# A hybrid layer on one core: norm weights on the gathered rows, another order of the last chunks' routing, overflow rows transposed one product later

## The chip, the cores and the metric

The kernel runs on one core of a Trainium2 chip. The metric is the device time of one execution in microseconds (us). A core has five engines, each with its own instruction queue: PE (TensorE, matrix products; PEld is its loading of the stationary operand), DVE (VectorE), ACT (ScalarE), POOL (GpSimd) and SP (SyncE, which here only starts transfers). ACT and POOL start transfers too. An engine works through its queue in order and waits on semaphores of the others.

## The reference

The input is 512 tokens of 1024 numbers. A normalized input goes through one combined projection into a stick-breaking attention and a gated spatial mix; both go through the output projection and are added to `h`. What the change touches is the second half:

```
hn = rmsnorm(h, ffn_norm_g)                 # h * rsqrt(mean(h*h)) * g
g_logits = hn @ w_router_group + b_g        # 4 groups: the best one
e_logits = hn @ w_router_expert + b_e       # 8 experts in it: the best two
h = h + sum over the token's two experts of
        gate * (silu(hn @ w_gate[e]) * (hn @ w_up[e])) @ w_down[e]
out = rmsnorm(h, final_norm_g)
```

There are 32 experts; `w_gate`, `w_up` and `w_down` hold 2 MB each per expert in float32, 201 MB in all.

## The kernel before

**Routing.** The tokens are four chunks `c` of 128 and `h[:, c]` is finished in two halves `n` by the output projection. The loop `for u in range(9)` does one half of one chunk per step and runs the letters of the string `U1[u]` in order, through `u_step`. The letters: `o` and `O` are the products of the output projection (tile `o`), `A` adds them to `h`; `q` squares the half before (`sqj`) and after its second half makes the row scale `rs2` (DVE, then a power on POOL); `t` transposes it on PE (`pt`) and ACT copies it out (`hT`); `l` is the product with the router weights (`lg`); `g` is `with_gain`, `h` times the norm weights `ffB`, on POOL and in step 8 on DVE; `s` is `store_xn`, which scales these rows by `rs2` on ACT and stores them to `xn_d` in DRAM; `r` and `R` run the next instructions of a chunk's routing on DVE (`route`: a chain of reductions over `L`, `em` to the two one-hot rows `oab`, at its end the `code` rows, on ACT for the last two chunks); `m`, `p`, `M` place the tokens (`pos_mm`, `positions`, `rows_mm`). After the loop the whole chain of chunk 3 runs (`go(16, R[3])`), gives the row list `gi`, and POOL gathers the first rows from `xn_d` into `xg`.

**Experts.** Sixteen pairs `p` of experts follow, 64 slots for each expert. For pair `p` PE does `gu(a)` and `gu(b)` (gate and up, tile `gu`), transposes the results (`act`, tile `ft`; ACT and DVE make `hg`), adds the pair before into `h` (`combine`, tiles `cb`), transposes the next pair's gathered rows (`prep_pair`, tiles `px`, evicted to `xs` by ACT and DVE), and does `down(p)` (tile `y`). Tokens beyond 64 of an expert, at most 32 in all, go through a second path: `over_2` gathers them into `xgo` in pair 0, `prep(xso, xgo, "o")` transposes them (`pxo`, to `xso`), and branches (`if_over`) use `xso` in the pairs that need it. At the end their sum `yo` is spread over the tokens with a one-hot tile `oho` and added in `unit`.

**What sets the order.** Each engine's order is the program's order. Weights come in 1 MB halves on SP's queue (`load_next`); a half can start when the slot that it takes is free, that is, when the products that read it last are done, and SP starts them strictly in order.

Of the kernel before, what the change touches and what calls it, by code (L numbers as in the profile page):

```python
# [8 lines left out]
F32 = mybir.dt.float32  # L9
F32R = mybir.dt.float32r  # L10
# [3 lines left out]
OP = mybir.AluOpType  # L14
# [39 lines left out]
)  # L54
U1 = (
# [9 lines left out]
)  # L65
F1 = 7
NSB = 4
# [4 lines left out]
def layer_kernel(ctx, tc, xr, xT, gT, w_inT, w_inR, sgg, wsT, bsp, sbg, sog, w_out, ffp, ffg, wr, br,  # L72
# [4 lines left out]
    def bcast(ap2d, cols):  # L77
        return bass.AP(tensor=ap2d.tensor, offset=ap2d.offset, ap=[[0, P], [1, cols]])
# [611 lines left out]
    dma(ffgs, ffg)  # L690
    brB = rw.tile([P, 36], F32, name="brB")
    dma(brB, bcast(br, 36))
    ffB = rw.tile([P, KD, P], F32, name="ffB")
    dma(ffB, bcast(ffp, D))
    load_next(2)
    slots[:0] = [half_slot(ringc)] * 4
    load_next(4)
# [35 lines left out]
        else:  # L733
            rsqrt(rs2[:, c:c + 1], msh[:, 1, c:c + 1], 1, msh[:, 0, c:c + 1])

    def with_gain(c, n, eng):

        if n == 0:
            xn[c] = rw.tile([P, KD, P], F32, tag="xn", bufs=2, name=f"xn{c}")
        ps_ = slice(n * 64, (n + 1) * 64)  # L740
        eng.tensor_tensor(xn[c][:, :, ps_], h[:, c, n * 512:(n + 1) * 512].rearrange("t (p k) -> t k p", k=KD),
                          ffB[:, :, ps_], op=OP.mult)

    def store_xn(c):
        nc.scalar.activation(xn[c], xn[c], AF.Copy, scale=rs2[:, c:c + 1])
        nc.scalar.dma_start(xn_d[c * P:(c + 1) * P], xn[c])

    def turn(c, n):
# [102 lines left out]
    def u_step(x, u):  # L851
        c, n = divmod(u, 2)
        pc, pn = divmod(u - 1, 2)
        if x == "o" and u < 8:
            bank1.append(op_.tile([P, 512], F32, tag="o", name=f"o1_{n}_{c}"))
            wo_mm(bank1[-1], 1, n, c, 0, 1)
        elif x == "O" and u < 8:
            wo_mm(bank1[-1], 1, n, c, 2, 3)
        elif x == "A" and u < 8:
            wo_add(bank1[-1], 1, n, c)  # L860
        elif x in "rR" and u >= 3:
            k = (8 if u >= 7 else 4) if x == "r" else 4
            go(k, R[(u - 3) // 2])
        elif x == "q" and u > 0:
            square(pc, pn)
        elif x == "t" and u > 0:
            turn(pc, pn)
        elif x == "g" and u > 0:
            with_gain(pc, pn, nc.vector if u == 8 else nc.gpsimd)
        elif x == "m" and u >= 5 and u != 6:  # L870
            pos_mm(2 if u == 8 else (u - 5) // 2)
        elif x == "p" and u in (5, 8):
            for k in (0,) if u == 5 else (1, 2):
                positions(k)
        elif x == "w" and u == 0:
            for k in range(KD):
                nc.vector.tensor_scalar(wrs[:, k], wrs[:, k], ffgs[:, k:k + 1], None, op0=OP.mult)
        elif x == "l" and u > 0:
            logits(pc, pn)
        elif x == "s" and u in (3, 5, 7):  # L880
            if u == 7:
                load_next(2)
            store_xn((u - 3) // 2)
        elif x == "M" and u in (6, 8):
            rows_mm(sps, soh, (0,) if u == 6 else (1, 2))
        elif x == "a":
            pass
# [72 lines left out]
    def prep(xs, x, name):  # L960

        for n in range(2):
            px = bank(f"px{name}_{n}", 4, P)
            for k in range(4):
                kk = 4 * n + k
                nc.tensor.transpose(px[:, k], x[:, kk * P:(kk + 1) * P], identf)  # L966
            (nc.scalar.copy, nc.vector.tensor_copy)[n](xs[:, 4 * n:4 * n + 4], px[:, :, :xs.shape[2]])

    def prep_pair(p):
        XS[p] = mo.tile([P, KD, P], F32, tag="xs", name=f"xs{p}")  # L970
# [75 lines left out]
    def combine(p, *units):  # L1046
        for u in units:
            ps = bank(f"cb{p}_{u}", 512)
            add_rows(ps, p, u, True, True)
            into_h(ps, u)  # L1050
# [109 lines left out]
    for p in range(NP):  # L1160
        a, b = 2 * p, 2 * p + 1
        last = p == NP - 1
        gu(a)
        if p == 0:
            over_1()
            pst = bank("pst", 2, NP)
            for i in range(8):
                for r, rs_ in halves:
                    nc.tensor.matmul(pst[rs_], ohf[:, i], cf[:, i, :, r::2], start=i == 0, stop=i == 7,
                                     skip_group_check=True)  # L1170
            nc.vector.tensor_copy(tab[:, 1], pst[:, 1])
            for c in range(NCH):
                nc.vector.tensor_scalar(tabt[:, c], pst[:, 0], PAD - c * P, None, op0=OP.add)
            load_next(4)
        if last:
            act(a)
            combine(p - 1, 0, 1, 2, 3, 4, 5)
        gu(b)
        if p == 0:
            over_2()  # L1180
            clear(True)
            load_next(4)
        else:
            with if_over(66 + p):  # L1184
                gate_up_over(a)
                gate_up_over(b)
            load_next(8)
        if last:
            act(b)
            combine(p - 1, 6, 7)  # L1190
            places(p)
            down_over(p)
            break
        act(a)
        if p:
            combine(p - 1, 0, 1, 2, 3)
        act(b)
        if p:
            combine(p - 1, 4, 5, 6, 7)
        places(p)  # L1200
        prep_pair(p + 1)
        if p == 0:
            prep(xso, xgo, "o")
        down(p)
        if p:
            down_over(p)
        load_next(4)
        results(p)


    room = [slots.pop(0)(f"fin{i}") for i in range(3)]
# [2 lines left out]
    dma(finB, bcast(fing, D))  # L1214
    p = NP - 1
    clear(False)
    oho = mo.tile([P, T], F32R, tag="cf", name="oho")
    for c in range(NCH):
        nc.vector.tensor_scalar(tabot[:, c:c + 1], tabo[:, :1], float(-c * P), None, op0=OP.add)
    tokens(oho, tabot)  # L1220
    yo2 = mo.tile([P, 2, 512], F32R, tag="xs", name="yo2")
    for n, rs_ in halves:
        nc.scalar.activation(yo2[:SLOTS, n], yo[rs_], AF.Copy, scale=tabo[rs_, 1:2])
# [13 lines left out]

    def unit(c, n):
        ps = bank(f"cl{c}_{n}", 512)
        nc.tensor.matmul(ps, oho[:, c * P:(c + 1) * P], yo2[:, n], start=True, stop=False, skip_group_check=True)  # L1240
        add_rows(ps, p, 2 * c + n, False, True)
        into_h(ps, 2 * c + n)

    def gained(c):
# [31 lines left out]
    def big(e, nm, oh2, tf, xr_, a, b):  # L1276
# [15 lines left out]
        for n in range(2):  # L1292
            px = bank(f"p2{nm}_{n}", 4, P)
            for k in range(4):
                kk = 4 * n + k
                for i in range(8):
                    nc.tensor.matmul(px[:, k], xr_[i % NCH][:, kk * P:(kk + 1) * P], own[:, i], start=i == 0,
                                     stop=i == 7, skip_group_check=True)
            nc.vector.tensor_copy(x2[:, 4 * n:4 * n + 4], px)
        pg = []  # L1300
        for i in range(2):
            ps = bank(f"g2{nm}_{i}", F)
# [69 lines left out]
def lay_out(x, attn_norm_g, w_in, sg_norm_g, w_spatial, b_spatial, sb_out_norm_g, sg_out_norm_g, w_out,  # L1372
            ffn_norm_g, w_router_group, b_router_group, w_router_expert, b_router_expert,
            w_gate, w_up, w_down, final_norm_g):
    import numpy as np
    c = np.ascontiguousarray

    def cols(v, n):
        return c(v.reshape(n, P).T)

    xs = x.reshape(T, D)
    wr = np.concatenate([w_router_group[0]] + [w_router_expert[0, g] for g in range(4)], axis=1)
    br = np.concatenate([b_router_group[0], b_router_expert[0].reshape(-1)])
    return {
        "xr": c(xs),
        "xT": c(xs.T.reshape(KD, P, T).transpose(1, 0, 2)),
        "gT": cols(attn_norm_g[0], KD),
        "w_inT": c(w_in[0].reshape(KD, P, 20, P).transpose(1, 2, 0, 3)[:, [0, 4, 1, 5, 2, 6, 3, 7, 12, 13, 14, 15]]),
        "w_inR": c(w_in[0].reshape(KD, P, 5, 512).transpose(1, 2, 0, 3)[:, [2, 4]]),
        "sgg": cols(sg_norm_g[0], NCH),  # L1390
        "wsT": c(w_spatial[0].transpose(2, 0, 1)),
        "bsp": c(b_spatial[0]),
        "sbg": cols(sb_out_norm_g[0], NCH),
        "sog": cols(sg_out_norm_g[0], NCH),
        "w_out": c(w_out[0].reshape(2, NCH, P, D).transpose(0, 2, 1, 3)),
        "ffp": c(ffn_norm_g[0].reshape(P, KD).T.reshape(1, D)),
        "ffg": cols(ffn_norm_g[0], KD),
        "wr": c(wr.reshape(KD, P, 36).transpose(1, 0, 2)),
        "br": c(br.reshape(1, 36)),
        "w_gate": c(w_gate.reshape(E, P, KD * F)),  # L1400
        "w_up": c(w_up.reshape(E, P, KD * F)),
        "w_down": c(w_down.reshape(E, P, 4 * D)),
        "fing": c(final_norm_g.reshape(1, D)),
    }
# [19 lines left out]
```

## Time and profile before

| What | Value |
|---|---|
| three runs | 756.58, 756.64, 760.25 us; median 756.64 |
| the profiled execution | 759.56 us, span 757.7 us |
| PE, busy share of the span | 93% |
| DVE, ACT, POOL | 41%, 29%, 12% |
| DMA | 231.54 MB, mean 306 GB/s |

The profile is of one execution, whose span (first to last instruction) is 1.86 us shorter than its time. Busy shares are means over stages with different limits. PE is nearly always busy, while the DMA engines are full only in the second two thirds of the span, where the page shows 418 to 420 GB/s in slice after slice.

### The profile page before, as it was taken

To read this page: it belongs to the slowest core of one execution; us is meant where nothing else is said; L and a number is where in the kernel's file an instruction comes from. 1 tells how busy PE (TensorE), PEld (TensorE's weight loads), DVE (VectorE), ACT (ScalarE), POOL (GpSimd) and SP (SyncE) were. 2 spreads that over 40 slices of the span, in tenths; PEclk is the share of its full clock that TensorE was granted. 3 is DMA by queue.
4 is the path that set the end of the run, shared out by engine and by line. 5 is a ranking of instruction groups with operands and counts; after the bars stand their busy time and mean duration, and the time that the engine had idled before them with its cause. 6 is when DMAs were issued, how large, how long until landed. Compare 5 with 4: busy or idle time off the path is not lost. (4 is left out here: it accounts for less than half of the span.)

```text
span 757.7 us, 9140 instructions
## 1 busy us (share of the span) xinstructions
PE 702.8 (93%) x3426; PEld 395.7 (52%) x3426; DVE 308.4 (41%) x541; ACT 216.5 (29%) x332; POOL 92.7 (12%) x84
## 2 busy tenths in 40 slices
PE   8999999999999796999999998989999999898993
PEld 6776757678788642434434434344344344244441
DVE  5546748355667711314304303042143043041355
ACT  6564856555344311111111111011111111111114
POOL 0322212125144201000000000000000000000001
PEclk9989979899999698999999999999999999999997
DMA  8802010207439597699999999999999999999953
GB/s 289 321 19 93 1 55 29 84 17 277 192 153 422 200 385 297 260 421 416 420 419 419 418 419 420 420 419 419 418 419 420 418 418 420 419 418 421 409 222 115
DMA packets 42391, 231.54 MB, mean 306 GB/s; under 512 B 6226, under 2 KB 7890, under 8 KB 18258
## 3 DMA queue, kind: packets, MB, share of 16 engines
q1 hardware_dynamic: 39394, 224.33, 73.1%
q0 software_dynamic: 2352, 4.20, 1.5%
q10 hardware_dynamic: 576, 2.10, 0.7%
q8 instruction: 43, 0.70, 0.4%
q14 instruction: 26, 0.21, 0.1%
HBM read 230.74 MB, written 4.19 MB: 310 GB/s over the span
## 5 line engine op out<-in xcount | busy, mean ns | idle before, releaser
L980 PE MATMUL gu<-r,xs 128*64 128x512 f32 x1024 | 226.1, 594 | 9.0 <-DMA r<-w_up 4.4
L980 PEld LDWEIGHTS gu<-r,xs 128*64 128x64 f32 x1024 | 82.8, 137 | 150.1 <-issue 137.2
L1010 PE MATMUL y<-r,hg 128*64 128x512 f32 x512 | 114.5, 600 | 3.3 <-ACTq L1145 2.9
L992 DVE TENSOR_TENSOR hg<-ft,gg 128x256 f32<-128x256 f32 x32 | 13.4, 420 | 231.5 <-ACT gg L990 224.4
L986 ACT COPY sg<-gu 128x512 f32<-128x512 f32 x32 | 18.7, 585 | 221.3 <-PE gu L980 221.3
L1044 DVE TENSOR_TENSOR h<-cb,h 128x512 f32<-128x512 f32 x120 | 74.2, 680 | 0.0
L1010 PEld LDWEIGHTS y<-r,hg 128*64 128x64 f32 x512 | 35.5, 138 | 71.6 <-issue 62.2
L918 POOL DMA_INDIRECT xg<-xn_d,gi x16 | 16.4, 1028 | 383.7 <-PE px L966 376.7
L1031 DVE SCALAR_TENSOR_TENSOR yl<-y,tab,yh 128x512 fp32r<-128x512 f32 x32 | 23.8, 750 | 71.0 <-ACT yh L1030 69.6
L1038 PE MATMUL cb<-yh,oh 128*128 128x512 f32 x120 | 49.9, 416 | 0.0
L1038 PE MATMUL cb<-yl,oh 128*128 128x512 f32 x120 | 47.4, 395 | 0.0
L1030 ACT ACTIVATE yh<-y,tab 128x512 fp32r<-128x512 f32 x32 | 21.8, 687 | 86.8 <-PE y L1010 86.1
L116 PE MATMUL pT<-xhi,hl_w 128*128 128x512 f32 x80 | 34.3, 429 | 0.0
L118 PE MATMUL pT<-xhi,hl_w 128*128 128x512 f32 x80 | 33.0, 413 | 0.0
L117 PE MATMUL pT<-xlo,hl_w 128*128 128x512 f32 x80 | 33.0, 412 | 0.0
L111 POOL TENSOR_TENSOR hl_w<-wqk,hl_w 128x1024 fp32r<-128x1024 f32 x10 | 24.4, 2435 | 66.5 <-ACT hl_w L110 64.2
L116 PE MATMUL pR<-hl_w,xhi 128*128 128x512 f32 x64 | 26.1, 409 | 0.0
L117 PE MATMUL pR<-hl_w,xhi 128*128 128x512 f32 x64 | 25.6, 400 | 0.2 <-DVE hl_w L111 0.2
L998 PEld LDWEIGHTS ft<-identf,sg 128*128 128x128 f32 x128 | 14.6, 140 | 21.3 <-issue 16.2
L118 PE MATMUL pR<-hl_w,xlo 128*128 128x512 f32 x64 | 25.4, 397 | 0.0
L1038 PEld LDWEIGHTS cb<-yh,oh 128*128 128x128 f32 x120 | 22.6, 188 | 4.8 <-DVE h L1044 0.8
L998 PE MATMUL ft<-identf,sg 128*128 128x128 f32 x128 | 19.6, 277 | 5.6 <-PEq L1184 3.7
(264 smaller groups left out, 941.3 us busy)
## 6 DMA issues: line engine op xcount, KB each, us to landing
r<-w_gate SPq DMA_DIRECT2D x64, 1024.0 KB, 20.0
r<-w_up SPq DMA_DIRECT2D x64, 1024.0 KB, 19.9
r<-w_down SPq DMA_DIRECT2D x64, 1024.0 KB, 20.2
wqk<-w_inT SPq DMA_DIRECT2D x10, 512.0 KB, 4.7
wr<-w_inR SPq DMA_DIRECT2D x8, 512.0 KB, 6.8
wo<-w_out SPq DMA_DIRECT2D x8, 512.0 KB, 4.5
xt<-xT SPq DMA_DIRECT2D x8, 256.0 KB, 4.5
h<-xr SPq DMA_DIRECT2D x4, 512.0 KB, 10.7
```

The source lines that it names most:

```text
L111: (nc.gpsimd if pool else nc.vector).tensor_tensor(lo, src, hi.bitcast(F32), op=OP.subtract)
L116: nc.tensor.matmul(ps, lh, rh, start=first, stop=False)
L117: nc.tensor.matmul(ps, lh, rl, start=False, stop=False)
L118: nc.tensor.matmul(ps, ll, rh, start=False, stop=last)
L980: nc.tensor.matmul(ps[rs_], xs[:, k], w, start=k == 0, stop=k == KD - 1, skip_group_check=True)
L986: nc.scalar.copy(SG[e], GU[e].rearrange("s (p j) -> s j p", j=4))
L998: nc.tensor.transpose(ft[:, j], SG[e][:, j], identf)
L1010: nc.tensor.matmul(YS[p][n][rs_], HT[e][:, j], down_weights(e, j, n), start=j == 0, stop=j == 3, skip_group_check=True)
L1030: nc.scalar.activation(yh[:, cs], YS[p][n], AF.Copy, scale=tab[:, 1, p:p + 1])
L1031: nc.vector.scalar_tensor_tensor(yl[:, cs], YS[p][n], tab[:, 1, p:p + 1], yh[:, cs].bitcast(F32), op0=OP.mult, op1=OP.subtract)
L1038: nc.tensor.matmul(ps, OHT[p][:, c * P:(c + 1) * P], y[:, n * 512:(n + 1) * 512], start=first and i == 0, stop=last and i == 1, skip_group ...
L1044: nc.vector.tensor_tensor(h[:, c, cs], ps, h[:, c, cs], op=OP.add)
```

## The change

Rows are now stored without the norm weights: `with_gain` (letter `g`) is gone, and ACT scales `h` straight into `xn`, earlier in steps 3, 5 and 7. The weights are multiplied in where the gathered rows leave PSUM after their transpose, where the weight is one number per partition (`ffk`): four activations per pair on ACT for the first half, one product with a broadcast operand on DVE for the second. The 512 KB broadcast `ffB` becomes 4 KB `ffk`. In step 8 the routing of chunk 2 goes first on DVE up to its one-hots (`z`), and its `code` rows on ACT come after the square and the copy (`k`). The overflow rows are transposed in pair 1 between `gu(a)` and `gu(b)`, and `oho` is made in pair 2; in `unit` its product is the last of three instead of the first.

```
-    "o r R q t g m p O A w l s M a",
-    "r R q t g a m p l M",
+    "o s r R q t m p O A w l M a",
+    "z q t m k p l M",
...
-    ffB = rw.tile([P, KD, P], F32, name="ffB")
-    dma(ffB, bcast(ffp, D))
+    ffk = keep.tile([P, KD], F32, name="ffk")
+    dma(ffk, ffp)
...
-        eng.tensor_tensor(xn[c][:, :, ps_], h[:, c, n * 512:(n + 1) * 512].rearrange("t (p k) -> t k p", k=KD),
-                          ffB[:, :, ps_], op=OP.mult)
...
-        nc.scalar.activation(xn[c], xn[c], AF.Copy, scale=rs2[:, c:c + 1])
+        xn[c] = rw.tile([P, KD, P], F32, tag="xn", bufs=2, name=f"xn{c}")
+        nc.scalar.activation(xn[c], h[:, c].rearrange("t (p k) -> t k p", k=KD), AF.Copy, scale=rs2[:, c:c + 1])
...
+        elif x == "z":
+            go(3, R[2])
+        elif x == "k":
+            go(1, R[2])
...
-            (nc.scalar.copy, nc.vector.tensor_copy)[n](xs[:, 4 * n:4 * n + 4], px[:, :, :xs.shape[2]])
+            if n == 0:
+                for k in range(4):
+                    nc.scalar.activation(xs[:, k], px[:, k, :xs.shape[2]], AF.Copy, scale=ffk[:, k:k + 1])
+            else:
+                nc.vector.tensor_tensor(xs[:, 4:], px[:, :, :xs.shape[2]],
+                                        ffk[:, 4:, None].to_broadcast([P, 4, xs.shape[2]]), op=OP.mult)
...
+        if p == 1:
+            prep(xso, xgo, "o")
         gu(b)
...
-        if p == 0:
-            prep(xso, xgo, "o")
         down(p)
...
+        if p == 2:
+            oho = mo.tile([P, T], F32R, tag="cf", name="oho")
+            for c in range(NCH):
+                nc.vector.tensor_scalar(tabot[:, c:c + 1], tabo[:, :1], float(-c * P), None, op0=OP.add)
+            tokens(oho, tabot)
...
-        nc.tensor.matmul(ps, oho[:, c * P:(c + 1) * P], yo2[:, n], start=True, stop=False, skip_group_check=True)
-        add_rows(ps, p, 2 * c + n, False, True)
+        add_rows(ps, p, 2 * c + n, True, False)
+        nc.tensor.matmul(ps, oho[:, c * P:(c + 1) * P], yo2[:, n], start=False, stop=True, skip_group_check=True)
```

On ACT, in step 8 of the routing loop, this stood before:

```order
L797 ACTIVATE code<-oab,tlocf 128x2x32
L798 ACTIVATE code<-oab 128x2x32
L729 ACTIVATE sqj,msh<-h 128x512
L754 COPY hT_1_1962<-pt_1_1957 128x512
L745 ACTIVATE xn_1924<-xn_1924,rs_1620 128x1024
L746 DMA xn_d<-xn_1924 128x1024
```

And this stands there now:

```order
L729 ACTIVATE sqj,msh<-h 128x512
L748 COPY hT_1_1952<-pt_1_1947 128x512
L791 ACTIVATE code<-oab,tlocf 128x2x32
L792 ACTIVATE code<-oab 128x2x32
L739 ACTIVATE xn_1987<-h,rs_1620 128x1024
L740 DMA xn_d<-xn_1987 128x1024
```

The two `code` rows of chunk 2 have moved behind the last square and the last copy; the store of chunk 3 reads `h` itself.

On PE, at the end of pair 0, this stood before, between the transposes of pair 1's rows and `down(0)`:

```order
L966 MATMUL px_1_2315<-identf,xg 128x128 x4
L966 MATMUL pxo_2324<-identf,xgo 128x128 x4
L966 MATMUL pxo_2330<-identf,xgo 128x128 x4
L1010 MATMUL y_0_2336<-r_2_0_1599,hg_2295 64x512
L1010 MATMUL y_0_2336<-r_2_0_1601,hg_2304 64x512
```

And now the overflow rows stand in pair 1, behind the last product of `gu(a)` and ahead of the first of `gu(b)`:

```order
L981 MATMUL gu_2354<-r_1_1_1892,xs_2303 64x512
L962 MATMUL pxo_2373<-identf,xgo 128x128 x4
L962 MATMUL pxo_2382<-identf,xgo 128x128 x4
L981 MATMUL gu_2388<-r_0_0_1985,xs_2303 64x512
L981 MATMUL gu_2388<-r_1_0_2063,xs_2303 64x512
```

The eight transposes are the same; `down(0)` and `gu(a)` of pair 1 now come before them. SP's order of weight halves is the same in both.

## Rows read from the trace of the kernel before

**Rows 1.** Busy time by stretch: PE, PEld, DVE, ACT, POOL, clock, DMA share, GB/s.

```profile
284.90:292.80 7.90, 1.88 (x10) 1.58 (x10) 1.61 (x3) 0.70 (x2) 1.59 (x2) 0.69 1.01 401
292.80:300.60 7.80, 7.80 (x33) 2.56 (x34) 0.29 (x1) 0.60 (x1) 0.00 (x0) 0.88 0.41 132
300.60:316.50 15.90, 15.59 (x76) 5.80 (x73) 2.07 (x4) 2.32 (x5) 0.00 (x0) 1.00 0.59 233
316.50:668.00 351.50, 335.53 (x1652) 150.40 (x1651) 99.92 (x172) 48.28 (x88) 11.87 (x12) 1.00 1.01 419
```

**Rows 2.** Timeline, pairs 1 and 14: start, duration, operation [wait before it].

```profile
314.67 0.33 SPq L592 DMA_DIRECT2D r<-w_up  x1
...
692.89 3.65 PE L980 MATMUL gu<-r,xs 128*64 128x512 f32 x14 [1.32 <-DMA r<-w_up]
```

**Rows 3.** Timeline, end of the routing loop, all engines.

```profile
247.11 1.57 POOL L741 TENSOR_TENSOR xn<-h,ffB 128x512 f32<-128x512 f32 x1 [1.37 <-DVE o_s L765]
247.20 1.51 DVE L791 TENSOR_SCALAR oab<-o_s,o_m 128x32 bf16<-128x32 f32 x1
...
247.60 0.98 PE L758 MATMUL lg<-wrs,hT 128*128 128x36 f32 x8
...
249.14 0.74 DVE L625 SCALAR_TENSOR_TENSOR h<-o,rb,h 128x512 f32<-128x512 f32 x1
...
250.30 0.24 DVE L791 TENSOR_SCALAR oab<-o_s,o_m 128x32 bf16<-128x32 f32 x1
...
250.97 0.58 ACT L729 ACTIVATE sqj<-h 128x512 f32<-128x512 f32 x1
...
251.59 0.56 ACT L754 COPY hT<-pt 128x512 f32<-128x512 f32 x1
...
252.20 1.92 PE L758 MATMUL lg<-wrs,hT 128*128 128x36 f32 x8 [1.31 <-ACT hT L754]
...
254.24 0.26 DVE L774 SCALAR_TENSOR_TENSOR L<-lg,rs,brB 128x36 f32<-128x36 f32 x1
254.49 0.33 ACTq L746 DMA_DIRECT2D xn_d<-xn  x1
...
259.99 1.28 POOL L918 DMA_INDIRECT xg<-xn_d,gi  x1 [6.71 <-DVE cov L934]
```

**Rows 4.** Timeline, pair 0 to pair 1, the overflow rows.

```profile
284.89 0.42 DVE L992 TENSOR_TENSOR hg<-ft,gg 128x256 f32<-128x256 f32 x1 [0.51 <-ACT gg L990]
...
290.92 1.94 PE L966 MATMUL pxo<-identf,xgo 128*128 128x128 f32 x8 [6.11 <-DMA xgo<-xn_d,gio]
292.05 0.27 ACT L967 COPY xso<-pxo 128x128 f32<-128x128 f32 x1 [6.71 <-PE pxo L966]
...
292.79 8.01 PE L1010 MATMUL y<-r,hg 128*64 128x512 f32 x32
```

**Rows 5.** Timeline, pair 14 to pair 15, eviction of the gathered rows.

```profile
701.46 1.03 PE L966 MATMUL px<-identf,xg 128*128 128x128 f32 x8
702.09 0.58 ACT L967 COPY xs<-px 128x512 f32<-128x512 f32 x1 [1.91 <-PE px L966]
702.73 7.09 PE L1010 MATMUL y<-r,hg 128*64 128x512 f32 x32 [0.24 <-ACTq L1145]
...
703.97 0.68 DVE L967 COPY xs<-px 128x512 f32<-128x512 f32 x1
...
710.13 7.09 PE L980 MATMUL gu<-r,xs 128*64 128x512 f32 x32 [0.31 <-PEq L1145]
```

**Rows 6.** Timeline, the last units.

```profile
737.52 2.75 DVE L1044 TENSOR_TENSOR h<-cl,h 128x512 f32<-128x512 f32 x4 [0.76 <-PE cl L1038]
...
743.39 0.50 PE L1038 MATMUL cl<-yl,oh 128*128 128x512 f32 x1 [0.69 <-DVE yl L1031]
```

**Rows 7.** DMA issues, stores of chunks 0 and 3: last column us to landing.

```profile
xn_d<-xn ACTq DMA_DIRECT2D x1, 512.0 KB, 8.3
...
xn_d<-xn ACTq DMA_DIRECT2D x1, 512.0 KB, 3.1
```

More of the change, by code (lines that the diff above doesn't have):

```diff
@@ L734, in square @@
             rsqrt(rs2[:, c:c + 1], msh[:, 1, c:c + 1], 1, msh[:, 0, c:c + 1])
[L736 to L740, printed above, removed]
-        eng.tensor_tensor(xn[c][:, :, ps_], h[:, c, n * 512:(n + 1) * 512].rearrange("t (p k) -> t k p", k=KD),
-                          ffB[:, :, ps_], op=OP.mult)
     def store_xn(c):
-        nc.scalar.activation(xn[c], xn[c], AF.Copy, scale=rs2[:, c:c + 1])
+        xn[c] = rw.tile([P, KD, P], F32, tag="xn", bufs=2, name=f"xn{c}")
+        nc.scalar.activation(xn[c], h[:, c].rearrange("t (p k) -> t k p", k=KD), AF.Copy, scale=rs2[:, c:c + 1])
         nc.scalar.dma_start(xn_d[c * P:(c + 1) * P], xn[c])
@@ L867, in u_step @@
             turn(pc, pn)
-        elif x == "g" and u > 0:
-            with_gain(pc, pn, nc.vector if u == 8 else nc.gpsimd)
+        elif x == "z":
+            go(3, R[2])
+        elif x == "k":
+            go(1, R[2])
         elif x == "m" and u >= 5 and u != 6:
@@ L1216, in layer_kernel @@
     clear(False)
[L1217 to L1220, printed above, removed]
     yo2 = mo.tile([P, 2, 512], F32R, tag="xs", name="yo2")
@@ L1298, in big @@
                                      stop=i == 7, skip_group_check=True)
-            nc.vector.tensor_copy(x2[:, 4 * n:4 * n + 4], px)
+            nc.vector.tensor_tensor(x2[:, 4 * n:4 * n + 4], px,
+                                    ffk[:, 4 * n:4 * n + 4, None].to_broadcast([P, 4, P]), op=OP.mult)
         pg = []
@@ L1395, in lay_out @@
         "w_out": c(w_out[0].reshape(2, NCH, P, D).transpose(0, 2, 1, 3)),
-        "ffp": c(ffn_norm_g[0].reshape(P, KD).T.reshape(1, D)),
+        "ffp": c(ffn_norm_g[0].reshape(P, KD)),
         "ffg": cols(ffn_norm_g[0], KD),
```

14 rows, old and new, of the table U1 are left out of this document.

## The prediction

> **What bounds the kernel now.** I read the busy time by stretch first. From 316.5 us to 668 us the DMA engines are full (share 1.01, 419 GB/s) and the clock is at its full 2.4 GHz; ahead of that stand two stretches in which the DMA engines are partly idle, 7.80 us at a share of 0.41 and 15.90 us at 0.59 [rows 1]. So they idle 7.80 x 0.59 + 15.90 x 0.41 = 4.6 + 6.5 = 11.1 us after the first experts have begun. The timeline says why: SP is ready, but its next weight half starts at 314.67 us, when `gu(b)` of pair 1 sets its slot free [rows 2]. The weight stream becomes gapless only from there. Late in the kernel, in pair 14, PE waits for a weight half, and only 1.32 us at the longest place [rows 2]. PE and the stream therefore run at nearly one pace: whatever brings PE to the end of pair 1 earlier brings the stream, and the end, earlier by as much, as long as some of the 11.1 us of idle DMA is left. Nothing that only makes an engine faster between pair 2 and pair 13 is worth much.
>
> Two places ahead of that point show PE waiting. The first is the end of the routing loop [rows 3], a chain over DVE, PE and ACT to the gather at 259.99 us. The second is pair 0: PE stands 6.11 us for the transfer of `xgo`, with `down(0)` queued behind it; the mean clock of that stretch is 0.69 [rows 1, 4].
>
> **The change, part by part.** *The routing's end.* Before, `oab` of chunk 2 takes 1.51 us, from 247.20 to 248.71, and POOL's `xn` runs from 247.11 to 248.68; the same DVE operation takes 0.24 us at 250.30 [rows 3]. The DVE operation ends 0.03 us behind POOL's: I read it as blocked by it. With `with_gain` gone, 1.51 - 0.24 = 1.27 us fall away, and `h` of the last half, behind it in DVE's queue, can start at 249.14 - 1.27 = 247.87. That is just after the product it needs: PE had gone on to `lg` at 247.60. It then ends at 248.61 instead of 249.88.
>
> Next the square. Before, ACT reaches it at 250.97, 1.09 us after `h` was ready, since chunk 2's `code` stood ahead and waited for chunk 2's one-hots, which DVE does after `h`. Now the square starts near 248.65, and the copy `hT` 0.62 us later as before, from 249.27 to 249.83. PE starts `lg` at 249.88. In step 8 `lg` took 1.92 us, in step 7 it took 0.98 [rows 3]: PE had been idle and its clock had gone to 1.2 GHz. With the long wait for `h` gone I take nearly the full clock; `L` follows 0.12 us after `lg`, so at 251.0 (full clock) or 251.9 (half), not at 254.24. DVE is no bar: what it does ahead of `L` follows the square, and the multiplication of step 8 is dropped from it. The gain is 3.2 or 2.3 us; I take 3.0. From `L` to the gather, 5.75 us [rows 3], nothing changes.
>
> The gather also needs the last store. It was issued at 254.49 and landed 3.1 us later, at 257.6 [rows 3, 7], 2.4 us before it was wanted. The store waits for the same square and moves with it, so that slack stays. The stores of chunks 0 to 2 go out earlier and have far more room.
>
> *The overflow rows.* Before, `down(0)` starts at 292.79 and takes 8.01 us, to 300.80. Its second operand `hg` is done at 285.31 [rows 4]. Without `pxo` in between it starts at 285.36 on this scale and takes the 7.09 us of a later pair [rows 5], since PE no longer stands idle long enough to lose its clock: it ends at 292.45, 8.35 us earlier. The eight transposes come back between `gu(a)` and `gu(b)` of pair 1, where `xgo` is long there: 1.03 us by the same form [rows 5] and some 0.1 for the switch, 1.94 us if the clock were low [rows 4]. Net 7.2 us, bounds 6.4 and 7.4. Who is late next: SP's half of 314.67 starts 10.2 us earlier, and the idle DMA time after pair 0's start shrinks from 11.1 to 11.1 - 7.2 = 3.9 us. The stream still waits for PE, so the gain arrives whole.
>
> *The evictions.* In each pair ACT now does four pieces of 128 elements instead of one of 512 (0.58 us). The nearest row is the 128-element copy, 0.27 us; four of them end to end are 1.08 [rows 4, 5]. In pairs 1 to 15 `down` covers this: ACT was done at 702.67, DVE at 704.65, and `gu` starts at 710.13 [rows 5], so 7.5 and 5.5 us are free; cost nothing. Without that cover it would be 0.5 us a pair. Pair 0 has no cover: if the first product needs only the first piece the change gives 0.3 us, if it needs all it costs 0.5. I take nothing. DVE's half is a product with a broadcast operand, which no row shows from PSUM; from 0.68 us as now to twice that, it lies inside the 5.5 us.
>
> Here a rule speaks against the change. The Trainium skill, "ScalarE: Activation LUTs", section "What ACT_TABLE_LOAD costs", gives an activation with one per-partition pointer operand about 280 ns plus 0.833 ns per element, with 93 ns of overlap between neighbours. An estimate from that page is 4 x 387 - 3 x 93 = 1270 ns for the four, so the sum would be 0.7 us worse in pair 0 if PE needed them all. The trace's 0.27 us for 128 elements, without such an operand, is below the page's figure.
>
> *The rest.* `oho` leaves the tail, but DVE waits 0.76 us for PE at the first unit anyway [rows 6], so this gives nothing; in pair 2 DVE has room. In the first unit of the second halves PE's last product waits for `yl` and runs at 743.39 [rows 6]; now one product more follows: at most its 0.50 us, pipelined about 0.2. The 512 KB of `ffB` go from a stream that idles later: nothing.
>
> **The sum.** -3.0 - 7.2 + 0.2 = -10.0 us. The profiled execution took 759.56 us (span 757.7 and 1.86 around it), so 749.6 by its measure. It is 2.9 us above the median of the runs, 756.64, which by the same sum becomes 746.6. The bounds of the terms (2.3 to 3.2; 6.4 to 7.4; pair 0's eviction -0.3 to +0.5; tail 0 to 0.5) give 745.7 to 748.9.
>
> **The rivals.** *The routing term is lost.* The gather then waits for the store. Chunk 0's store, issued while weights filled the DMA engines, took 8.3 us to land, chunk 3's, in an idle stretch, 3.1 [rows 7]. If the store now falls among the last weight halves it lands up to 5.2 us later, 2.8 us beyond its slack: -10.0 + 2.8, 749.4. For it: the store moves toward the weights. Against: those halves were issued before the loop's end and drain anyway. The Trainium skill, "DMA: Bandwidth & Descriptors", section "Queues, rings and completion order", says that each DMA engine takes packets in turn from the queues that have work; by that rule a store beside the stream is slowed as chunk 0's row shows, without stopping.
>
> *The DMA stream takes the second term back.* If it were already the bound from pair 0 on, only the routing's 3.0 us would arrive: 753.6. For it: the share of 1.01 through the middle. Against: 11.1 us of idle DMA behind the very wait that is removed.
>
> *Slower.* The new evictions come after `down` ends, and PE waits in every pair. The place is `xs` ahead of `gu`; the point from which it decides is DVE's half taking 5.5 us more than its 0.68. To eat the 10.0 us, the 15 covered pairs must lose 0.67 us each beyond that; at 1 us each the time is 756.64 - 10.0 + 15 = 761.6. Nothing in the rows comes near.
>
> **Chances and range.** The forecast 0.72, the routing term lost 0.14, the stream as the bound 0.07, slower 0.03, something unplaced 0.04. Runs of one kernel here lie up to 3.7 us apart (756.58 to 760.25), and about 0.5%, 3.8 us, is what a measurement can tell from no change. The likeliest is 746.6, which I round to 746.8 for the runs' skew upward; 744.5 to 751.5 holds the forecast and the first rival with that scatter. Faster by over 0.5% (below 752.9): 0.88; within: 0.08; slower: 0.04.
>
> **What would show it.** Right: DVE's `oab` in step 7 at 0.24 us; `lg` of step 8 at about 1 us; the gather near 257.0; no wait for `xgo`; `down(0)` at 7.1 us right behind the second `hg`; SP's half of 314.67 near 304.5; the DMA engines full from about 306. Wrong: a wait of the gather or of ACT on `xn_d`; PE waiting for weights in pairs 2 to 10; `gu` waiting for `xs`; or a weight stream that starts earlier and ends no earlier.

## The result and the profile after

The changed kernel took 746.43, 747.23, 748.78 and 752.61 us, median 748.0; the kernel before, on the same chip, 758.0 (four runs). The ratio is 0.9865, 95% interval 0.9826 to 0.9905. Forecast were 746.8 us and a range of 744.5 to 751.5. The profiled execution is the longest of the four, 752.61 us with a span of 750.6.

The page of the changed kernel hides where the time came from: its first 250 us are 2 us *longer* than before, in code that the change hardly touches. The view by stretch of the two kernels shows PE's granted clock there (column PEclk) falling at other times in each execution. From 60 to 90 us, before and now:

```profile
60.00:90.00 30.00, 28.16 (x127) 19.73 (x125) 19.80 (x20) 18.37 (x21) 7.04 (x3) 1.00 0.11 36
60.00:90.00 30.00, 28.23 (x100) 18.90 (x99) 16.07 (x15) 16.27 (x18) 5.98 (x3) 0.77 0.10 36
```

So all times below are counted from one mark behind that stretch: the start of the group `lg` in step 7 of the routing loop, at 247.60 us before [rows 3] and at 249.76 now. The loop ahead of the mark kept its length: from the first `lg` group, in step 1, to the mark it is 25.26 us before and 25.29 now.

**The routing's end.** Timeline of the changed kernel, all engines (start, duration, operation, wait before it):

```profile
248.40 0.24 DVE L785 TENSOR_SCALAR oab<-o_s,o_m 128x32 bf16<-128x32 f32 x1
...
249.76 0.97 PE L752 MATMUL lg<-wrs,hT 128*128 128x36 f32 x8
249.96 0.75 DVE L625 SCALAR_TENSOR_TENSOR h<-o,rb,h 128x512 f32<-128x512 f32 x1 [0.81 <-PE o L118]
...
250.80 0.60 ACT L729 ACTIVATE sqj<-h 128x512 f32<-128x512 f32 x1 [1.64 <-DVE h L625]
...
252.15 1.08 PE L752 MATMUL lg<-wrs,hT 128*128 128x36 f32 x8 [0.56 <-ACT hT L748]
...
252.43 2.16 ACT L739 ACTIVATE xn<-h,rs 128x1024 f32<-128x1024 f32 x1
...
253.35 0.26 DVE L768 SCALAR_TENSOR_TENSOR L<-lg,rs,brB 128x36 f32<-128x36 f32 x1 [0.24 <-PE lg L752]
...
254.62 0.33 ACTq L740 DMA_DIRECT2D xn_d<-xn  x1
...
258.61 0.17 DVE L841 SCALAR_TENSOR_TENSOR gi<-sps,stl 128x16 int32<-128x16 f32 x1
...
259.67 1.28 POOL L914 DMA_INDIRECT xg<-xn_d,gi  x1 [7.26 <-DVE tot L933]
```

Two rows of the kernel before belong beside it, the scaling of the same rows and the row list:

```profile
253.31 1.15 ACT L745 ACTIVATE xn<-xn,rs 128x1024 f32<-128x1024 f32 x1 [1.16 <-POOL rs L177]
...
259.50 0.17 DVE L847 SCALAR_TENSOR_TENSOR gi<-sps,stl 128x16 int32<-128x16 f32 x1
```

Beside [rows 3]: `oab` is at 0.24 us, the square follows `h` by 0.09 us instead of 1.09, `lg` takes 1.08 instead of 1.92, and `L` stands 3.59 us behind the mark instead of 6.64, 3.05 earlier. In the stretch of that `lg` the granted clock (third column from the end) was 0.50 before and is 1.00 now, which are the two levels 1.2 and 2.4 GHz:

```profile
252.20:254.10 1.90, 1.90 (x10) 1.83 (x12) 1.76 (x11) 0.79 (x1) 1.08 (x1) 0.50 0.59 244
252.15:253.23 1.08, 1.08 (x12) 1.04 (x14) 0.89 (x6) 1.08 (x3) 0.25 (x1) 1.00 1.03 432
```

But from `L` to the gather there are 6.32 us, not 5.75 (0.89 us from the end of `gi` to the gather instead of 0.32), and the scaling of the last stored rows takes 2.16 us instead of 1.15.

**The overflow rows.** PE of the changed kernel from the end of pair 0 on, which answers to [rows 4], and one row of SP:

```profile
283.39 1.04 PE L962 MATMUL px<-identf,xg 128*128 128x128 f32 x8
284.36 7.28 PE L1011 MATMUL y<-r,hg 128*64 128x512 f32 x31
...
298.86 1.09 PE L962 MATMUL pxo<-identf,xgo 128*128 128x128 f32 x8
299.88 2.37 PE L981 MATMUL gu<-r,xs 128*64 128x512 f32 x10
...
307.10 0.33 SPq L592 DMA_DIRECT2D r<-w_up  x1
```

The wait for `xgo` is gone, `down(0)` follows at once, and the eight transposes come back at 1.09 us. SP's half of [rows 2], the last row here, starts 57.34 us behind the mark instead of 67.07. The stretches of [rows 1], with the columns given there:

```profile
292.00:300.00 8.00, 8.00 (x42) 4.72 (x40) 1.48 (x3) 1.72 (x5) 0.00 (x0) 1.00 1.01 420
300.00:304.00 4.00, 4.00 (x20) 1.36 (x22) 0.28 (x1) 0.37 (x3) 0.00 (x0) 1.00 0.86 358
304.00:308.00 4.00, 3.69 (x20) 1.42 (x17) 0.00 (x0) 0.64 (x2) 0.00 (x0) 1.00 0.03 8
308.00:316.00 8.00, 8.00 (x44) 4.99 (x44) 6.74 (x12) 1.85 (x6) 0.99 (x1) 1.00 0.98 383
316.00:660.00 344.00, 329.62 (x1604) 144.49 (x1601) 93.47 (x163) 52.69 (x118) 10.89 (x11) 0.99 1.01 419
```

The DMA engines still idle 4.00 x 0.14 + 4.00 x 0.97 + 8.00 x 0.02 = 4.6 us behind the first experts, instead of 11.1.

**The evictions** of pair 14, which answer to [rows 5]:

```profile
694.04 1.04 PE L962 MATMUL px<-identf,xg 128*128 128x128 f32 x8
694.68 1.14 ACT L965 ACTIVATE xs<-px,ffk 128x128 f32<-128x128 f32 x4 [1.91 <-PE px L962]
695.00 7.09 PE L1011 MATMUL y<-r,hg 128*64 128x512 f32 x32
696.55 0.68 DVE L967 TENSOR_TENSOR xs<-px,ffk 128x512 f32<-128x512 f32 x1
702.41 2.79 PE L981 MATMUL gu<-r,xs 128*64 128x512 f32 x12 [0.31 <-PEq L1146]
```

ACT takes 1.14 us instead of 0.58, DVE 0.68 as before, and `gu` (its group is cut by the window here) starts 5.18 us after DVE has ended.

### The profile page after: what moved, and what is told of

It is laid out like the page before. It is cut to its first block, busy times and chain, and to the rows that moved or that the text cites. A ratio compares the mean times of both kernels' runs of the same rounds, so it can differ in the third digit from the quotient of the medians.

```text
span 750.6 us, 9187 instructions
## 1 busy us (share of the span) xinstructions
PE 706.2 (94%) x3426; PEld 400.1 (53%) x3426; DVE 303.8 (40%) x540; ACT 230.1 (31%) x383; POOL 81.0 (11%) x77
## 5 line engine op out<-in xcount | busy, mean ns | idle before, releaser
L981 PE MATMUL gu<-r,xs 128*64 128x512 f32 x1024 | 229.5, 598 | 9.0 <-DMA r<-w_up 4.7
L981 PEld LDWEIGHTS gu<-r,xs 128*64 128x64 f32 x1024 | 86.2, 138 | 149.9 <-issue 131.6
L116 PE MATMUL pT<-xhi,hl_w 128*128 128x512 f32 x80 | 35.2, 440 | 0.0
L118 PE MATMUL pT<-xhi,hl_w 128*128 128x512 f32 x80 | 33.7, 421 | 0.0
L965 ACT ACTIVATE xs<-px,ffk 128x128 f32<-128x128 f32 x64 | 18.2, 368 | 32.5 <-PE px L962 32.5
```

Source lines behind the costliest of these rows:

```text
L116: nc.tensor.matmul(ps, lh, rh, start=first, stop=False)
L118: nc.tensor.matmul(ps, ll, rh, start=False, stop=last)
L965: nc.scalar.activation(xs[:, k], px[:, k, :xs.shape[2]], AF.Copy, scale=ffk[:, k:k + 1])
L981: nc.tensor.matmul(ps[rs_], xs[:, k], w, start=k == 0, stop=k == KD - 1, skip_group_check=True)
```

## The experiments

Executions of one kernel lie 3 to 10 us apart, most of it from the first 250 us: the mark falls between 243.0 and 251.0 us in the profiled executions. So the medians tell the large term, and the small ones are read from the distances in each run's own timeline. Starts of `L` of chunk 3, of the first gather and of the first `gu`, and the end of the last output product (`fin` on DVE), all in us behind the mark; `gi` to gather is from the end of `gi`:

| Kernel | median, us | mark at | L | gi to gather | gather | first gu | end |
|---|---|---|---|---|---|---|---|
| before | 757.5 | 247.60 | 6.64 | 0.32 | 12.39 | 18.02 | 502.77 |
| changed | 748.0 | 249.76 | 3.59 | 0.89 | 9.91 | 15.48 | 493.10 |
| changed_again | 748.1 | 244.35 | 3.60 | 0.91 | 9.93 | 15.89 | 493.53 |
| overflow_back | 755.4 | 248.97 | 3.59 | 0.89 | 9.91 | 16.00 | 501.22 |
| overflow_alone | 752.4 | 246.16 | 6.63 | 0.31 | 12.36 | 17.94 | 495.59 |
| code_first | 750.9 | 244.49 | 4.47 | 0.88 | 10.78 | 16.40 | 493.94 |
| pool_busy | 749.0 | 243.09 | 3.69 | 0.32 | 9.43 | 15.50 | 492.89 |
| store_step_written | 747.3 | 244.03 | 3.59 | 0.88 | 9.89 | 15.88 | 493.36 |
| rows_in_order | 749.0 | 243.04 | 3.60 | 0.89 | 9.92 | 15.39 | 492.88 |
| store_twice | 748.3 | 244.41 | 3.59 | 1.63 | 10.65 | 15.96 | 493.50 |
| gather_fewer_waits | 750.5 | 243.54 | 3.59 | 1.23 | 10.25 | 15.77 | 493.36 |
| gather_same_waits | 750.2 | 250.97 | 3.60 | 0.89 | 9.91 | 15.95 | 493.47 |
| tail_back | 748.6 | 243.17 | 3.59 | 1.04 | 10.07 | 15.59 | 492.84 |
| evict_twice | 748.4 | 247.13 | 3.60 | 0.89 | 9.91 | 15.93 | 493.47 |

The kernel before had a median of 757.5 us beside the runs down to `store_twice`, and of 761.0 beside the last four. The column "first gu" also holds 0.3 to 0.4 us that are not the change's: the first transposes `px` took 1.09 us in the changed kernel's first profile and 1.42 in `changed_again`, at granted clocks of 1.00 and 0.77.

**changed_again**: no edit, the mark for the rest.

> The changed kernel once more, as the mark for the runs beside it. Expected 747 to 749 us, 10.0 us below the kernel before. By the theory of the late store the first gather again starts about 0.9 us after its row list gi is written (0.3 before the change); if that was chance of one execution, 0.3.

Ratio 0.9885 (0.9817 to 0.9954). The 0.9 us between `gi` and the gather is there again: not chance.

**overflow_back** and **overflow_alone**: the changed kernel with the overflow rows transposed in pair 0 again, and the kernel before with that move alone. The first edit:

```
-        if p == 1:
-            prep(xso, xgo, "o")
         gu(b)
...
         prep_pair(p + 1)
+        if p == 0:
+            prep(xso, xgo, "o")
         down(p)
```

> The changed kernel with the overflow rows transposed in pair 0 again, everything else as changed. Theory (PE stands for the transfer of xgo, and the weight stream follows PE): the 6 us wait and the slow down(0) of 8.0 us come back, and the time rises by 7.2 us to about 755. Rival (the weight stream is the bound from pair 0 on): it rises by less than 1 us.

> The kernel before with this one edit alone: the overflow rows transposed in pair 1, between gu(a) and gu(b). Theory: 7.2 us less than the kernel before, about 750.8. Rival (the stream as the bound): less than 1 us. If both terms add, this gain and the 3 us of the rest make 10.

With the rows moved back the wait and the slow `down(0)` are there again:

```profile
290.11 1.94 PE L962 MATMUL pxo<-identf,xgo 128*128 128x128 f32 x8 [5.94 <-DMA xgo<-xn_d,gio]
291.98 8.58 PE L1011 MATMUL y<-r,hg 128*64 128x512 f32 x32
```

Ratios to the kernel before: 0.9974 (0.9935 to 1.0013) with the rows moved back, 0.9936 (0.9900 to 0.9972) with the move alone. By its median the move alone gives 5.0 us instead of the 7.2 expected, with an interval from 2.1 to 7.6: too wide to size it. From the first `gu` to the end it is 484.75 us before, 477.62 in the changed kernel, 485.22 with the rows moved back and 477.65 with the move alone: 7.6 us lost by undoing it (`down(0)` took 8.58 us there, not 8.01, which is about the difference), 7.1 won by doing it alone. The rival (the weight stream as the bound) is refuted in both directions. The move alone also keeps the routing's end as it was (`L` at 6.63). At the end of the kernel the move alone is 7.18 us ahead of the kernel before and the rest alone (`overflow_back`) 1.55, in sum 8.7, against 9.2 and 9.7 for both: the terms add to within 1 us.

**code_first**: chunk 2's `code` rows ahead of the last square on ACT, `with_gain` still gone.

```
-    "z q t m k p l M",
+    "z k q t m p l M",
```

> The changed kernel with chunk 2's code rows ahead of the last square on ACT again, the multiplication on POOL still gone. Theory: ACT waits for chunk 2's one-hots, the square starts about 1.2 us later (at 1.3 us behind h's end instead of 0.1), the router product, L, the store and the gather follow; the time rises by 1.2 us, or by 2.1 if PE's clock falls meanwhile and lg takes 1.9 us instead of 1.1. Rival (taking the multiplication off POOL gave the whole routing term): no change, below 0.3 us.

`L` comes at 4.47 instead of 3.59 or 3.60, the gather 0.9 us later and `gu` 0.5 to 0.9 later. The order is worth 0.9 us, less than the 1.2 expected, and taking `with_gain` away the other 6.64 - 4.47 = 2.17. ACT's wait alone did not slow `lg`: PE stood 1.43 us for it, and `lg` still took 1.08 us at a granted clock of 1.00. The rival (order worth nothing) falls. Ratio 0.9925 (0.9894 to 0.9957), by itself too wide to tell.

**pool_busy**: a multiplication put back on POOL in step 7 (letter `g`, with a tile `ffB` of ones).

```
...
+            nc.gpsimd.tensor_tensor(ffB[:, :, :64], h[:, pc, pn * 512:(pn + 1) * 512].rearrange("t (p k) -> t k p", k=KD),
+                                    ffB[:, :, 64:], op=OP.mult)
```

> The changed kernel with a multiplication put back on POOL in step 7, at the old place and of the old shape, on data that nobody uses. Theory (DVE stands while POOL works): oab of chunk 2 takes about 1.5 us instead of 0.24, h of the last half ends up to 1.3 us later, and the time rises by 0.5 to 1.3 us (h starts 0.8 us after PE's product in the changed kernel, so not all of it need arrive). Rival (oab was long for another reason): oab 0.24 us, no change.

`oab` stayed at 0.24 us and `L` lost only 0.1. The reason is the place: nothing held the operation back, while `with_gain` had waited for the store out of its buffer (its row in `overflow_alone`, further below), so POOL ran it 3.0 us earlier against the mark than in [rows 3]. There it shows the block all the same. Timelines of DVE and POOL in this run:

```profile
239.59 1.67 POOL L865 TENSOR_TENSOR ffB<-h,ffB 128x512 f32<-128x512 f32 x1 [1.00 <-DVE h L625]
...
240.06 1.22 DVE L761 SCALAR_TENSOR_TENSOR og_s<-L,gm,desc 128x4 f32<-128x4 f32 x1
241.31 0.16 DVE L728 TENSOR_REDUCE og_m<-og_s 128x1 f32<-128x4 f32 x1
```

and the same instruction in `changed_again`, where POOL is idle:

```profile
241.32 0.22 DVE L759 SCALAR_TENSOR_TENSOR og_s<-L,gm,desc 128x4 f32<-128x4 f32 x1
```

A DVE operation on four numbers takes 1.22 us instead of 0.22 and ends 0.02 us after POOL's. This is the place where the half before had its `with_gain`, and the kernel before shows the same block there:

```profile
244.07 1.67 POOL L741 TENSOR_TENSOR xn<-h,ffB 128x512 f32<-128x512 f32 x1
...
244.62 1.13 DVE L765 SCALAR_TENSOR_TENSOR og_s<-L,gm,desc 128x4 f32<-128x4 f32 x1
```

So DVE was blocked twice before, by 0.91 us here and by 1.27 at `oab`. In the changed kernel it waits 0.81 us for PE ahead of `h`, and that takes up most of one block: with the block of this run `h` starts 0.31 us behind the mark instead of 0.20, with both blocks, before, 1.54. Mechanism confirmed; what the block at `oab` costs by itself this run does not test. The Trainium skill, "SBUF — State Buffer", section "Who interferes with whom", says that DVE and GpSimd share one pair of ports as an exclusive lock, and that a DVE instruction with two SBUF inputs contends with a GpSimd instruction that reads SBUF; by that rule, the trace agrees.

**store_step_written**, **rows_in_order** and **store_twice**: is it the longer scaling of chunk 3's rows that delays the gather? The first writes with the step, the second does without one (the transposes then pick every eighth column), the third does the activation twice. The second's edit:

```
-        nc.scalar.activation(xn[c], h[:, c].rearrange("t (p k) -> t k p", k=KD), AF.Copy, scale=rs2[:, c:c + 1])
+        nc.scalar.activation(xn[c].rearrange("t k p -> t (p k)"), h[:, c], AF.Copy, scale=rs2[:, c:c + 1])
...
-                nc.tensor.transpose(px[:, k], x[:, kk * P:(kk + 1) * P], identf)
+                nc.tensor.transpose(px[:, k], x[:, kk::KD], identf)
...
```

> The changed kernel; the activation that scales h into the stored rows reads h in order and writes with a step of 512 bytes, instead of reading with a step of 32 bytes and writing in order. Theory (the strided read made it 2.16 us instead of 1.15): about 1.15 us, the last store is issued 1 us earlier, the gather follows gi by 0.3 us instead of 0.9, and the time falls by 0.6 us. Rival (any step costs, read or written): 2.2 us, and nothing changes.

> The changed kernel with rows stored in h's own order, read and written without a step; the transposes of the gathered rows pick every eighth column instead (a step of 32 bytes on PE). Theory: the store's activation takes 1.15 us, the gather follows gi by 0.3 us, the time falls by 0.6 us, and the transposes cost what they did (8 in 1.0 to 1.1 us). Rival (PE pays for the step too): transposes at twice the time, which in 16 pairs costs up to 16 us where PE and the stream run at one pace.

> The changed kernel with the activation that makes chunk 3's stored rows done twice. Theory (the first gather waits for that store): the gather starts 2.2 us later against gi, 3.1 instead of 0.9 us behind it, and the time rises by 2.2 us. Rival (0.9 us is the gather's own start, or DVE's tot): below 0.3 us. Rival (a slack of 2.4 us stays, as the prediction had it): no change at all.

Writing with a step takes 2.08 us, as long as reading with one: the rival was right there. Without any step the scaling is back at 1.15 us and the store goes out 1 us earlier, and still the gather follows `gi` by 0.89 us; 0.3 was expected. So the strided activation is not what holds the first gather in the changed kernel. The second run's rival, that PE pays for the step, falls: eight transposes took 1.05 to 1.06 us in the later pairs, against 1.03 to 1.04 in the changed kernel. With the activation done twice, 2.1 us more, the gather comes 0.72 us later: there the store seems to decide, after some 1.4 us of slack are used up (its landing is not in the trace). No ratio of these three differs from that of the changed kernel (0.9882, 0.9903, 0.9892, intervals of 0.004 to 0.005 to each side).

Why an earlier store gives nothing shows in the landing of chunk 3's store (last column, us from issue), first of `rows_in_order`'s relative `gather_same_waits` (below), then of the changed kernel:

```profile
xn_d<-xn ACTq DMA_DIRECT2D x1, 512.0 KB, 5.0
```

```profile
xn_d<-xn ACTq DMA_DIRECT2D x1, 512.0 KB, 3.3
```

The last weight half ahead of it is issued 1.8 us ahead of the mark in all of them. The store goes out 8.7 us after that half in the kernel before and needs 3.1 us [rows 7], 6.7 us after it in the changed kernel (3.3 us, and 4.2 in `tail_back`), and 5.7 us after it with rows in order (5.0, and 5.4 in `gather_fewer_waits`). Between its issue and its landing the DMA engines moved 0.55 MB before, 0.66 in the changed kernel, 1.28 and 1.45 with rows in order, of which the store is 0.52. So, issued earlier, it shares them with more of the weights and lands no earlier: 8.2 and 9.1 us behind the mark in the changed kernel and `tail_back`, 8.9 and 9.3 with rows in order.

**gather_fewer_waits** and **gather_same_waits**: what else could the 0.57 us be? As built, the first gather of the changed kernel waits for six semaphores, POOL's own among them (its early clearing of `xg`); in the kernel before for three, in `pool_busy` for five, neither with POOL's own. Both runs have rows in order; the first makes POOL see its clearing early, the second has two like instructions that don't.

```
...
     nc.gpsimd.memset(xg, 0.0)
+    pk = early.tile([P, 2], F32, name="pk")
+    nc.gpsimd.tensor_tensor(pk[:, :1], xg[:, :1], xg[:, :1], op=OP.mult)
+    nc.gpsimd.tensor_tensor(pk[:, 1:], pk[:, :1], pk[:, :1], op=OP.mult)
...
```

> Rows stored in h's order, and two tiny chained operations on POOL (one number per partition) right behind the early clearing of xg, so that POOL has already seen its own clearing done: the first gather then waits for five semaphores instead of six, POOL's own being the sixth. Theory (the sixth wait, which stands behind the wait for gi, costs the 0.57 us): gather 0.3 us behind gi instead of 0.9, and with the shorter store about 0.6 us less time than the changed kernel. Rival (POOL starts late because it stood idle for 7 us, or for its place in the instruction stream): 0.9 us as in the other runs, no change.

> The control of the run beside it: rows stored in h's order, and two tiny operations on POOL at the same place that do not touch xg and do not hang on each other, so that the gather keeps its six waits. Theory of the sixth wait: 0.9 us from gi to the gather. Rival (the place in POOL's instruction stream, moved by two instructions): 0.3 us here too.

The control is at 0.89 us, but the run that should have come to 0.3 came to 1.23, so it decides nothing: its store landed at 247.39 + 5.4 = 252.8 us, and the gather started 1.0 us later.

```profile
247.39 0.33 ACTq L743 DMA_DIRECT2D xn_d<-xn  x1
...
253.79 1.29 POOL L917 DMA_INDIRECT xg<-xn_d,gi  x1 [7.61 <-DVE cnt L1106]
```

In `tail_back`, too, the gather starts 1.0 us after the store's landing, 1.04 us behind `gi` instead of 0.89, so there the store decides; in `gather_same_waits` it lands as long ahead of the gather, but `gi` ends later still, and the usual 0.89 us show. In the changed kernel the gather starts 1.75 us after the landing (254.62 + 3.3 = 257.92; 259.67), so there the store does not decide. Three kernels without POOL's semaphore in the wait show 0.31 to 0.32 us. That fits the sixth wait, but the test of it failed.

One account fits all nine kernels whose landing of that store the trace has. As built, the gather waits for one semaphore itself, and for the others instructions of their own wait just ahead of it in POOL's queue. The wait for the store stands ahead in all kernels. The wait for `gi` stands on the gather in the kernel before, `overflow_alone`, `pool_busy` and `gather_fewer_waits`; in the other ten POOL's own semaphore, long there, has that place, and `gi` is waited for ahead. What comes last ahead of the gather is followed by it after 0.9 to 1.1 us, what comes last at the gather itself after 0.3. By this the 0.57 us would come from the place of the wait for `gi`. But the place and the number of the waits change together in every run here, so this is not shown, and what the 0.57 us is stays open.

**tail_back**: `oho` made in the tail again, its product first in `unit`, both as in the kernel before.

> The changed kernel with the tail as before: oho is made at the end again, and its product is the first of three in each unit. By the prediction's +0.2 us for the tail: from the start of the last gu to the end of the last output product 29.1 us as before the change, instead of 29.3. Rival (oho in the tail costs DVE time ahead of the first unit): 29.5 us or more.

From the start of the last `gu` to the end: 29.10 us before, 29.32 in the changed kernel, 29.31 in `changed_again`, 29.10 here. The tail's price is 0.21 us, and making `oho` in the tail costs nothing. The rival falls.

**evict_twice**: every eviction of gathered rows done twice in pairs 1 to 15.

```
-                for k in range(4):
+                for k in list(range(4)) * (1 if name in (0, "o") else 2):
...
+              for _ in range(1 if name in (0, "o") else 2):
...
```

> The changed kernel with every eviction of gathered rows done twice in pairs 1 to 15: eight pieces on ACT, two products on DVE, ahead of gu. Theory (down covers them, 5 us and more are free): no change, below 0.5 us over all pairs. Rival (gu waits for them, or DVE and ACT are late for what follows): 0.7 us or more a pair, 10 us and up.

The pieces are done twice, in pair 14 as in the others:

```profile
692.27 2.17 ACT L965 ACTIVATE xs<-px,ffk 128x128 f32<-128x128 f32 x8 [1.91 <-PE px L962]
692.60 7.09 PE L1012 MATMUL y<-r,hg 128*64 128x512 f32 x32
694.15 1.41 DVE L968 TENSOR_TENSOR xs<-px,ffk 128x512 f32<-128x512 f32 x2
700.14 3.23 PE L982 MATMUL gu<-r,xs 128*64 128x512 f32 x14 [0.46 <-PEq L1147]
```

From the first `gu` to the end it is 477.54 us, against 477.62 and 477.64: no cost, with 4.6 us still free behind DVE. The rival of 10 us and more is refuted.

None of these kernels beats the changed one by more than the scatter; the lowest in the end column, `tail_back`, `rows_in_order` and `pool_busy`, are 0.2 to 0.7 us below it, and their medians are not.

## Why the prediction was right

**The overflow term**, -7.2 us. Right in mechanism and size: -7.1 as the only edit, -7.6 by undoing it. `down(0)` took 7.28 us against 7.09, the transposes 1.09 against about 1.1, and 4.6 us of idle DMA stayed instead of 3.9. That some idle was left is the point: the stream still waited for PE, so the gain arrived whole, as the 11.1 us of [rows 1] said.

**The routing term**, -3.0 us. To `L` it is 3.05. The steps also hold one by one: `h` ends 1.33 us earlier (1.27 said, for the block at `oab`; the other one, of 0.91, is mostly taken up by DVE's wait for PE), the square sits right behind it, `lg` runs at 1.08 us. One attribution was loose. The 0.9 us of `lg` were put down to PE's clock, and DVE was called no bar because its own product falls away. Both were needed, for in the kernel before the two ended together. In `overflow_alone`, which has that kernel's routing, `lg` took only 1.38 us at a granted clock of 0.73 and was over at 252.19, and DVE still reached `L` at 252.79, its product of 1.08 us in the way. Timeline of that run:

```profile
245.73 1.56 POOL L741 TENSOR_TENSOR xn<-h,ffB 128x512 f32<-128x512 f32 x1 [1.40 <-DMA xn_d<-xn]
245.80 1.52 DVE L791 TENSOR_SCALAR oab<-o_s,o_m 128x32 bf16<-128x32 f32 x1
...
250.45 1.08 DVE L741 TENSOR_TENSOR xn<-h,ffB 128x512 f32<-128x512 f32 x1
...
252.58 0.29 DVE L821 TENSOR_TENSOR soh<-slotf,pos 128x128 bf16<-128x128 f32 x1
252.79 0.25 DVE L774 SCALAR_TENSOR_TENSOR L<-lg,rs,brB 128x36 f32<-128x36 f32 x1
```

A faster clock alone would have brought nothing. The two rows ahead of it show `oab` blocked as in [rows 3]: it ends 0.03 us behind POOL.

**"From `L` to the gather, 5.75 us, nothing changes"** and **"that slack stays"**. This is the step that failed. It is 6.32 us, and of the 3.05 won at `L` 12.39 - 9.91 = 2.48 reach the gather. The store did move with the square, but its scaling became 1.0 us longer, because it now reads `h` with a step, an operation that the prediction took at its old length. And the store came 2 us closer to the last weight half, the rival with 0.14: where it lands late (4.2 us in `tail_back`, 5.4 in `gather_fewer_waits`) it sets the gather, at most 0.9 us behind where `gi` would have allowed it, not the 2.8 worked out. So a sign named as wrong, a wait of the gather on `xn_d`, did appear in `tail_back`, whose routing is the changed kernel's, and cost 0.15 us. In the changed kernel's own profile the store does not decide, and the cause of the 0.57 us is open. The size of the miss, 0.6 us of 10, lies inside the range for either cause.

**The evictions**, 0. Right for pairs 1 to 15, as `evict_twice` shows with double the work. In pair 0 `gu` starts 1.21 us after `px` instead of 1.39 (264.23 to 265.62 us before): the first piece is enough, a gain of 0.2 within the bounds given, at full clock. Of the two prices for four pieces, 1.08 from the 128-element row and an estimated 1270 ns from the Trainium skill, "ScalarE: Activation LUTs", section "What ACT_TABLE_LOAD costs", the trace's 1.14 us lies nearer the row.

**The tail**, +0.2. Measured 0.21.

**The sum.** Behind the mark the changed kernel gains 502.77 - 493.10 = 9.67 us in one profile and 9.24 in the other, against 10.0 predicted: 0.6 was lost at the gather and 0.2 won at pair 0's eviction, and in the second profile PE's lower clock at the first `px` took 0.3 more. The medians differ by 10.0 and 9.4 us (758.0 to 748.0, and 757.5 to 748.1). That the first is 10.0 to the decimal is luck: its interval reaches from 7.2 to 13.2 us. The forecast of 746.8 was 1.2 us low mainly because it started from a median of 756.64, which a fourth execution brought to 758.0.

## What to carry to other kernels

Where a transfer that is needed later stands in an in-order queue between two pieces of ready work, moving it behind the second piece gains the whole wait, as long as the resource that runs beside (here the weight stream) still idles for that engine; read its idle time first, since that is the ceiling. When an edit changes an operand's layout, price the operation anew in every place where it stands: dropping a multiplication also made the copy read with a step. And take small terms from distances between rows of one execution behind the noisy stretch, not from medians that scatter by more than the term.

## What the hardware showed unasked

- ACT took 1.15 us to scale 128x1024 float32 in order, 2.13 to 2.31 reading them with a step of 32 bytes, and 2.08 to 2.11 writing with a step of 512 bytes. PE's transposes with a step of 32 bytes took 1.05 to 1.06 us for eight beside 1.03 to 1.04 (in pair 0, 1.16 beside 1.09), at full clock.
- POOL's power of one number per partition took 1.27 us instead of 0.55 while DVE worked on its 1.08 us product: the block goes both ways.
- A 512 KB store issued 1 us earlier behind the same weight half took 5.0 to 5.4 us to land instead of 3.3 to 4.2, and landed no earlier.
- An indirect gather on POOL started 0.31 to 0.32 us after its row list was written in three kernels, and 0.88 to 0.91 in the eight whose wait for the list stands ahead of it and whose store was not late.
